# The first stage of an encoder layer: silu's row and the inverse norm in PSUM, three of four latent blocks, the rotary tables and the distances behind the loop

## The chip, the cores and the metric

The kernel runs on one core of a Trainium2 chip. The time is the device time of one execution in microseconds; three executions were measured, and one more was recorded by the hardware profiler. A core has a matrix engine (PE), a vector engine (DVE), an activation engine (ACT), a general engine (POOL) and an engine that issues most DMAs (SP); each works through its own queue of instructions in order, and semaphores tie them together. Data lie in SBUF; PE writes into PSUM, here eight banks of 128 x 512 floats.

## The reference, cut to what matters

Two layers of an encoder on 512 tokens of width 1024, all in float32:

```python
c_act = silu(c)
for l in range(DEPTH):
    mod = c_act @ w_mod[l] + b_mod[l]
    sh1, sc1, gt1, sh2, sc2, gt2 = split(mod, 6)
    h = rms_norm(x, g_norm_mix[l]) * (1 + sc1) + sh1
    q_d, k_d, v_d, cq, ckv, k_rope = split(h @ w_in[l], cuts)
    o_dil = dilated_attention(rms_norm(q_d), rms_norm(k_d), v_d, positions, slopes)   # 8 heads
    o_mla = latent_attention(cq, ckv, k_rope, positions, ...)                         # 8 heads
    x = x + gt1 * (concat([o_dil, o_mla]) @ w_out[l])
    h = rms_norm(x, g_norm_mlp[l]) * (1 + sc2) + sh2
    x = x + gt2 * (relu(h @ w_mlp_in[l]) ** 2 @ w_mlp_out[l])
```

## The kernel before

A product of two float32 matrices is made of three matmuls (`mm3`, L237 to L240): both factors are split into a high and a low half, and high x high, low x high and high x low are added up in PSUM. The high half is a copy on ACT; the low half is the difference, mostly on POOL. `load_split` (L228) does this for weights: a DMA into a "raw" or "zz" tile, ACT's copy (L233, tile wh), POOL's subtraction (L234, tile wl).

Activations lie transposed: x is eight tiles of 128 features by 512 tokens. The projection `w_in` is cut into four pairs of dilated heads, PR[0] to PR[3] (384 columns each), and W, the latent projection (416 columns: query latent, key-value latent, rotary key). Each is done in four blocks of 128 tokens (`tb`), over eight feature tiles (`k`): 24 matmuls of 128x384 or 128x416 to a block.

The first stage, up to the first scores, stands in the code under `if l == 0`, and does four things. (1) silu(c) is spread to all partitions by two matmuls and copied to SBUF as `cb` (L118). (2) The squares of x are added up (tile o), a matmul with ones gives the sum in all partitions, and `inv_rms` makes the inverse norm y in SBUF. (3) A loop over k = 0 to 7 makes column k of the modulation by two multiplications of a 128x1024 weight block with cb, summed along the row (`mod_block`, L170, DVE, one block in a "qk" and one in an "ot" tile), then u = x * y (L706 or L715, DVE, tile pt), its high half h (L719, ACT), the modulated u (L720, ACT) and the low half of h (L722 on POOL for odd k, L710 on DVE for even k); then PE does the step k of PR[0] into four banks named mm, and of W into four named sc and tr: 24 matmuls to a step. (4) Behind the loop stand the chains: norms of q and k of PR[0] (ACT L435, L222, L223, L446; DVE L436, L224 to L226, L443, L447), the same for the latent (ACT L508; DVE L510 to L512), the transposes of both (L455, L523), and the distances between positions for the linear bias (DVE L312 to L322, ACT L321).

Then come eight stages of heads, two heads each. In the first four, a head and block of 128 queries has its scores on PE (L468, L469, bank sc), the softmax with bias on DVE (L343) and ACT (L344, L351), the bias made on ACT (L338) and POOL (L339), the normalisation on POOL (L355) or ACT, transposes on PE (L358, bank tr) and the product with values (L368). The projection of the next pair and its loads and splits are woven in between.

The program is written with a list scheduler that puts each engine's instructions into an order from a simulated time line; where the code names an engine in `manual_schedule` (before: DVE, in the loop alone) or calls `keep_in_program_order`, the order is that of the code. Tiles come from pools with a fixed number of buffers to a name: a new tile waits for the readers of the one whose buffer it takes.

Of the kernel before, what the change touches and what calls it, by code (L numbers as in the profile page):

```python
# [9 lines left out]
F32 = mybir.dt.float32  # L10
# [6 lines left out]
L = 2  # L17
D = 1024
# [24 lines left out]
def trunk(ctx: ExitStack, tc: tile.TileContext, a):  # L43
# [7 lines left out]
    psum = ctx.enter_context(tc.tile_pool(name="psum", bufs=1, space=bass.MemoryType.PSUM))  # L51
# [4 lines left out]
    def nm(p):  # L56
# [5 lines left out]
                mm=4, sc=2, tr=2)  # L62
# [10 lines left out]
    def ps(tag, shape=(128, 512)):  # L73
        return psum.tile(list(shape), F32, tag=tag, bufs=BUFS[tag], name=nm(tag))
# [12 lines left out]
    SY.dma_start(cs, a["c"].rearrange("(k p) -> p k", p=128))  # L87
    ident = const.tile([128, 128], F32, name="ident")
    SY.dma_start(ident, a["ident"])
    cols = [col(N_COL, f"cols{l}") for l in range(L)]  # L90
    SY.dma_start(cols[0], a["cols"][0])
    posc = const.tile([128, 4], I32, name="posc")
    SY.dma_start(posc, a["pos"].rearrange("(t p) -> p t", p=128))
    inv = col(16, "inv")
    SY.dma_start(inv, bass.AP(tensor=a["inv"].tensor, offset=a["inv"].offset, ap=[[0, 128], [1, 16]]))

    xT = [const.tile([128, S], F32, name=f"x{j}") for j in range(8)]
    for j in range(8):
        SY.dma_start(xT[j], a["xT"][j])
    ones = const.tile([128, 128], F32, name="ones")  # L100
# [10 lines left out]
    cb = const.tile([128, D], F32, name="cb")  # L111
    for i in range(2):
        p = ps("sc", (128, 4, 128))
        dg = s2([128, 4, 128])
        for k in range(4):
            V.tensor_scalar(dg[:, k], ident, cs[:, 4 * i + k:4 * i + k + 1], None, op0=OP.mult)
        T.matmul(p.rearrange("p k c -> p (k c)"), ones, dg.rearrange("p k c -> p (k c)"), start=True, stop=True)
        A.activation(cb[:, 512 * i:512 * i + 512], p.rearrange("p k c -> p (k c)"), AF.Copy)  # L118
# [814 lines left out]
```

## Time and profile before

| | |
|---|---|
| median of three executions | 1374.31 us (1374.08 to 1374.61) |
| profiled execution | 1371.87 us, its span 1370.1 us |
| PE busy | 1274.0 us, 93% of the span |
| DVE, ACT, POOL busy | 762.4, 683.7 and 662.0 us |
| mean granted clock | 0.974 |

The profile gives for one execution every instruction with its start, its duration and what ended the idle time before it. The numbers of the instructions' tiles are left out there, so `mm` is any bank of that name; a line (L234) is one of the program above, and may be that of a helper that many parts call. In the lines of the timeline the first column is the start in us, the second the duration (several like instructions in a row are one line, with their count at the end).

### The profile page before, as it was taken

The numbers are of one execution on the slowest core, as the hardware profiler recorded it, in microseconds if no ns is written. First come the engines' busy times: TensorE is split into PE (matmuls) and PEld (weight loads), VectorE is DVE, ScalarE is ACT, GpSimd is POOL, SyncE is SP. The second block draws the span as 40 slices with busy tenths as digits, with TensorE's granted clock in tenths as the row PEclk, the third lists the DMA queues.
The fourth block names the chain that finished last, engine by engine and source line by source line (L and its number), as shares of the span: only waits on it lengthen the run. The fifth ranks groups of instructions, "written<-read, shape, count | busy, mean of one in ns | idle before, by whom it ended". The sixth has DMA issues, their size and how long they took to land.

```text
span 1370.1 us, 19443 instructions
## 1 busy us (share of the span) xinstructions
PE 1274.0 (93%) x6922; PEld 1106.1 (81%) x6922; DVE 762.4 (56%) x1732; ACT 683.7 (50%) x1453; POOL 662.0 (48%) x600
## 2 busy tenths in 40 slices
PE   3889878888999999999998999899889999999999
PEld 2877867777988888888888999788788888888888
DVE  6687887786653481743576577998562122121223
ACT  5578787876442231322235577888654233232321
POOL 5646686663454444444436244455246444444441
PEclk7989998999999999999999999999999999999999
DMA  9325553232235483754533244311013223222321
GB/s 344 112 88 184 165 160 101 87 108 73 98 123 185 149 280 108 235 203 133 181 124 89 89 122 145 93 47 47 17 62 106 94 93 101 99 92 97 104 92 62
DMA packets 57248, 167.61 MB, mean 122 GB/s; under 512 B 8640, under 2 KB 10816, under 8 KB 57152
## 3 DMA queue, kind: packets, MB, share of 16 engines
q1 hardware_dynamic: 57152, 166.38, 37.3%
q8 instruction: 54, 0.88, 0.3%
q14 instruction: 42, 0.34, 0.1%
HBM read 155.87 MB, written 10.49 MB: 121 GB/s over the span
## 4 chain that ended last, share of the span: by engine, by line
PE 73%; DVE 6%; ACT 6%; issue 4%; POOL 3%; DMA 3%; POOLq 0%; DVEq 0%; ACTq 0%
PE mm L238 21%; PE mm L239 21%; PE mm L240 21%; PE tr L368 2%; PE tr L358 2%; POOL wl L234 2%; DMA raw<-in_wout_dram 1%; DVE pt L362 1%; DVE raw L170 1%; DMA raw<-in_wup_dram 1%; ACT pt L361 1%; PE sc L238 1%; ACT P L347 1%; PE mm L603 1%; PE sc L239 1%
## 5 line engine op out<-in xcount | busy, mean ns | idle before, releaser
L234 POOL TENSOR_TENSOR wl<-raw,wh 128x1024 fp32r<-128x1024 f32 (+3 forms) x188 | 425.7, 2268 | 454.9 <-ACT wh L233 433.1
L233 ACT ACTIVATE wh<-raw 128x1024 fp32r<-128x1024 f32 (+3 forms) x188 | 188.7, 1004 | 272.6 <-PE mm L240 202.7
L636 DVE SCALAR_TENSOR_TENSOR x<-mm,mod,x 128x512 f32<-128x512 f32 (+1 forms) x144 | 89.3, 630 | 261.7 <-PE mm L240 261.2
L238 PE MATMUL mm<-h,wh 128*128 128x512 f32 (+1 forms) x608 | 224.5, 370 | 7.1 <-ACT h L274 7.1
L239 PE MATMUL mm<-h,wl 128*128 128x512 f32 (+1 forms) x608 | 224.4, 370 | 0.0
L240 PE MATMUL mm<-h,wh 128*128 128x512 f32 (+1 forms) x608 | 222.1, 369 | 1.6 <-POOL h L271 1.1
L238 PE MATMUL mm<-ot,wh 128*128 128x512 f32 (+1 forms) x448 | 155.2, 348 | 4.3 <-ACT ot L628 4.1
L239 PE MATMUL mm<-ot,wl 128*128 128x512 f32 (+1 forms) x448 | 154.0, 345 | 0.0
L240 PE MATMUL mm<-ot,wh 128*128 128x512 f32 (+1 forms) x448 | 152.6, 347 | 0.2 <-POOL ot L629 0.2
L809 ACT ACTIVATE P<-mm 128x512 f32<-128x512 f32 (+1 forms) x72 | 39.2, 551 | 203.2 <-PE mm L240 203.2
L238 PEld LDWEIGHTS mm<-h,wh 128*128 128x128 f32 x608 | 116.1, 191 | 25.9 <-ACT h L274 7.5
L240 PEld LDWEIGHTS mm<-h,wh 128*128 128x128 f32 x608 | 114.6, 190 | 21.1 <-POOL h L271 1.5
L239 PEld LDWEIGHTS mm<-h,wl 128*128 128x128 f32 x608 | 116.1, 191 | 19.1 <-POOL wl L234 0.3
L810 DVE SCALAR_TENSOR_TENSOR mm<-mm,P 128x512 f32<-128x512 f32 (+1 forms) x72 | 45.4, 635 | 139.5 <-ACT P L809 139.5
L238 PE MATMUL mm<-wh,h 128*128 128x384 f32 (+1 forms) x288 | 97.0, 352 | 16.5 <-ACT h L719 9.8
L238 PE MATMUL mm<-qk,wh 128*128 128x512 f32 (+1 forms) x288 | 105.2, 366 | 1.0 <-DVE x L636 1.0
L239 PE MATMUL mm<-qk,wl 128*128 128x512 f32 (+1 forms) x288 | 105.2, 365 | 0.0
L240 PE MATMUL mm<-qk,wh 128*128 128x512 f32 (+1 forms) x288 | 105.2, 365 | 0.0
L239 PE MATMUL mm<-wh,h 128*128 128x384 f32 (+1 forms) x288 | 99.8, 349 | 5.3 <-POOL h L722 3.2
L240 PE MATMUL mm<-wl,h 128*128 128x384 f32 (+1 forms) x288 | 99.3, 347 | 0.8 <-POOL wl L234 0.8
L170 DVE SCALAR_TENSOR_TENSOR pt<-pt,cb 128x1024 f32<-128x1024 f32 x56 | 99.2, 1806 | 0.0
L238 PEld LDWEIGHTS mm<-ot,wh 128*128 128x128 f32 x448 | 85.3, 190 | 15.2 <-ACT ot L628 4.5
(248 smaller groups left out, 2673.3 us busy)
## 6 DMA issues: line engine op xcount, KB each, us to landing
raw<-in_w_dram SPq DMA_DIRECT2D x64, 512.0 KB, 3.4
pt<-in_wmod_dram SPq DMA_DIRECT2D x56, 512.0 KB, 4.9
raw<-in_w2a_dram SPq DMA_DIRECT2D x48, 512.0 KB, 3.5
raw<-in_wmod_dram SPq DMA_DIRECT2D x24, 512.0 KB, 3.7
raw<-in_win_dram SPq DMA_DIRECT2D x30, 384.0 KB, 3.1
bias<-b SPq DMA_DIRECT2D x32, 256.0 KB, 2.3
raw<-in_wout_dram SPq DMA_DIRECT2D x16, 512.0 KB, 3.7
raw<-in_w2b_dram SPq DMA_DIRECT2D x16, 512.0 KB, 3.3
```

What stands on the lines that cost most here:

```text
L170: r = V.scalar_tensor_tensor(w, w, 1.0, cb, op0=OP.mult, op1=OP.mult, accum_out=out)
L233: A.activation(hi, raw, AF.Copy)
L234: G.tensor_tensor(lo, raw, f(hi), op=OP.subtract)
L238: T.matmul(out, sh, mh, start=first, stop=False)
L239: T.matmul(out, sl, mh, start=False, stop=False)
L240: T.matmul(out, sh, ml, start=False, stop=last)
L347: A.activation(P, sc, AF.Exp, bias=m, scale=1.0, accum_out=l_)
L358: T.transpose(tr[:, kc], P[:, kc * 128:(kc + 1) * 128], ident)
L368: T.matmul(po[:, HALF[qh]], vals(hd, kc), pt[qh][w][:, kc], start=(kc == 0 and w == 0), stop=(kc == 3 and w == 1))
L636: V.scalar_tensor_tensor(xT[j][:, hf], p, gt[:, j:j + 1], xT[j][:, hf], op0=OP.mult, op1=OP.add)
L809: A.activation(r, p, AF.Relu)
L810: V.scalar_tensor_tensor(p, p, 0.0, r, op0=OP.max, op1=OP.mult)
```

## The change

silu's row stays in its two PSUM banks (`cbp`) and is copied to SBUF behind the loop only, by two copies on ACT (L763 of the changed kernel). The inverse norm stays in a bank "y". So the multiplications for the modulation (now L716) and u = x * y (L747) read one operand from PSUM. The sum of squares runs in PSUM as well, and two of the eight squares go to POOL. The banks of the first stage are a pool of its own, closed behind the loop, and a second pool with the old names is opened after that.

With two banks for cb, one for y and four for PR[0], one bank is left for the latent projection: in the loop only its block 0 is done, 15 matmuls to a step in place of 24. The other three blocks, 72 matmuls, stand behind the loop. All sixteen modulation blocks are loaded into eight "qk" tiles; four latent weight halves lie in "ot" tiles. All low halves of h are made on POOL. In the loop the order on SP, DVE, ACT and POOL is that of the code.

Five small loads are issued from ACT's queue; the arithmetic of the rotary angles goes from POOL to DVE; the split of positions into high and low parts moves to the start of the program. The distances use ACT and, in place of one DVE instruction, two on POOL (L329, L330), behind the loop and ahead of the first latent chain. PR[1]'s first two loads with their splits, and the rotary tables, come behind the latent blocks.

```diff
-    psum = ctx.enter_context(tc.tile_pool(name="psum", bufs=1, space=bass.MemoryType.PSUM))
+    start = ExitStack()
+    psum = [start.enter_context(tc.tile_pool(name="psum0", bufs=1, space=bass.MemoryType.PSUM))]
...
+                mm=4, sc=2, tr=2, cb=1, y=1, w=2, lat=1)
...
+    posc = const.tile([128, 4], I32, name="posc")
+    A.dma_start(posc, a["pos"].rearrange("(t p) -> p t", p=128))
+    inv = col(16, "inv")
+    A.dma_start(inv, bass.AP(tensor=a["inv"].tensor, offset=a["inv"].offset, ap=[[0, 128], [1, 16]]))
+    posr = s2([128, S], I32, tag="o")
+    A.dma_start(posr, bass.AP(tensor=a["pos"].tensor, offset=a["pos"].offset, ap=[[0, 128], [1, S]]))
...
-    cb = const.tile([128, D], F32, name="cb")
-    for i in range(2):
-        p = ps("sc", (128, 4, 128))
-        dg = s2([128, 4, 128])
-        for k in range(4):
-            V.tensor_scalar(dg[:, k], ident, cs[:, 4 * i + k:4 * i + k + 1], None, op0=OP.mult)
-        T.matmul(p.rearrange("p k c -> p (k c)"), ones, dg.rearrange("p k c -> p (k c)"), start=True, stop=True)
-        A.activation(cb[:, 512 * i:512 * i + 512], p.rearrange("p k c -> p (k c)"), AF.Copy)
...
+    cbp = ps("cb", (128, D))
+    for i in range(2):
+        dg = s2([128, 4, 128], tag="P")
+        for k in range(4):
+            V.tensor_scalar(dg[:, k], ident, cs[:, 4 * i + k:4 * i + k + 1], None, op0=OP.mult)
+        T.matmul(cbp[:, 512 * i:512 * i + 512], ones, dg.rearrange("p k c -> p (k c)"), start=True, stop=True)
...
+    def split(raw, n, tags=("wh", "wl"), keep=False):
+        hi, lo = t4(tags[0], [128, 1024])[:, :n], t4(tags[1], [128, 1024])[:, :n]
+        ra = A.activation(hi, raw, AF.Copy)
+        rg = G.tensor_tensor(lo, raw, f(hi), op=OP.subtract)
+        if keep:
+            tc.keep_in_program_order(ra)
+            tc.keep_in_program_order(rg)
+        return hi, lo
...
+    def distances(row, clm):
         dist = [t4("ot", [128, 2, S], F32) for _ in range(2)]
         for qb in range(4):
             d = dist[qb // 2][:, qb % 2]
-            A.activation(d, row[:, 0], AF.Identity, bias=clm[:, 0, qb:qb + 1], scale=65536.0)
-            V.scalar_tensor_tensor(d, row[:, 1], clm[:, 1, qb:qb + 1], d, op0=OP.subtract, op1=OP.add)
+            tc.keep_in_program_order(A.activation(d, row[:, 0], AF.Identity, bias=clm[:, 0, qb:qb + 1], scale=65536.0))
+            u = s2()
+            G.tensor_scalar(u, row[:, 1], clm[:, 1, qb:qb + 1], 0.0, op0=OP.subtract, op1=OP.add)
+            G.tensor_tensor(d, d, u, op=OP.add)
...
+            blocks(w, W_C, step, chain, 1 if l == 0 else 0)
...
-            lbanks = [ps("sc") for _ in range(2)] + [ps("tr") for _ in range(2)]
...
+            def mods(k):
+                ml[8 + k] = mod_load(0, 8 + k, "qk")
+                ml[k] = mod_load(0, k, "qk")
...
+            def splits(i):
+                PR[0]["put"](i, *split(wr[i][0], 768))
+                W["put"](i, *split(wr[i][1], 2 * W_C, ("ot", "ot") if i < 2 else ("wh", "wl")))
+            def mod_mul(i):
+                V.scalar_tensor_tensor(ml[i], ml[i], 1.0, cbp, op0=OP.mult, op1=OP.mult, accum_out=mraw[:, i:i + 1])
...
+            with tc.manual_schedule(engines={E.SP, E.DVE, E.Activation, E.Pool}):
...
+                sq0, sqp = s2(tag="o"), ps("lat")
+                A.activation(sqp, xT[0], AF.Square)
+                for j in range(1, 8):
+                    sq = s2(tag="P")
+                    if j in (1, 4):
+                        G.tensor_tensor(sq, xT[j], xT[j], op=OP.mult)
+                    else:
+                        A.activation(sq, xT[j], AF.Square)
+                    V.tensor_tensor(sq0 if j == 7 else sqp, sqp, sq, op=OP.add)
+                T.matmul(p, ones, sq0, start=True, stop=True)
...
+                for k in range(8):
+                    u = us[k // 2][:, k % 2]
+                    hi, lo = hh[k // 2][:, k % 2], hl[k // 2][:, k % 2]
+                    ga, be = amix[0][:, k:k + 1], modc[0][:, k:k + 1]
+                    V.tensor_tensor(u, xT[k], p, op=OP.mult)
+                    first_norm(k)
+                    A.activation(hi, u, AF.Identity, bias=be, scale=ga)
+                    A.activation(u, u, AF.Identity, bias=be, scale=ga)
+                    G.tensor_tensor(lo, u, f(hi), op=OP.subtract)
+                    if k % 2 == 0 and k < 6:
+                        splits(k // 2 + 1)
                     if k < 7:
-                        if k >= 0:
-                            V.tensor_tensor(u_of(k + 1), xT[k + 1], y, op=OP.mult)
-                        mod_block(0, 9 + k, "qk", out=mraw[:, 9 + k:10 + k])
-                    if k >= 0 and k % 2 == 0:
-                        hi, lo = h_of(k)
-                        V.tensor_tensor(lo, u_of(k), f(hi), op=OP.subtract)
-                    if k < 7:
-                        mod_block(0, k + 1, "ot", out=mraw[:, k + 1:k + 2])
-                        if k < 0:
-                            inv_rms(p, v, y, t)
-                            V.tensor_tensor(u_of(0), xT[0], y, op=OP.mult)
-                        first_norm(k + 1)
-                        hi, lo = h_of(k + 1)
-                        ga, be = amix[0][:, k + 1:k + 2], modc[0][:, k + 1:k + 2]
-                        A.activation(hi, u_of(k + 1), AF.Identity, bias=be, scale=ga)
-                        A.activation(u_of(k + 1), u_of(k + 1), AF.Identity, bias=be, scale=ga)
-                        if k % 2 == 0:
-                            G.tensor_tensor(lo, u_of(k + 1), f(hi), op=OP.subtract)
-                    if k >= 0:
-                        for tb in range(4):
-                            PR[0]["step"](banks[tb][:, :384], k, tb)
-                        for tb in range(4):
-                            W["step"](lbanks[tb][:, :W_C], k, tb)
-            gains()
+                        mod_mul(9 + k)
+                        mod_mul(k + 1)
+                    for tb in range(4):
+                        PR[0]["step"](banks[tb][:, :384], k, tb)
+                    W["step"](lbank[:, :W_C], k, 0)
...
             for tb in range(4):
                 PR[0]["do_chain"](tb, banks[tb])
-            for fn in PR[1]["load"][:2]:
-                fn()
-            for tb in range(4):
-                W["do_chain"](tb, lbanks[tb])
+            for i in range(2):
+                tc.keep_in_program_order(A.activation(cb[:, 512 * i:512 * i + 512], cbp[:, 512 * i:512 * i + 512], AF.Copy))
+            bias0 = distances(*parts)
+            W["do_chain"](0, lbank)
+            start.close()
+            psum[0] = ctx.enter_context(tc.tile_pool(name="psum", bufs=1, space=bass.MemoryType.PSUM))
+            for tb in range(3):
+                for fn in W["mm"][tb]:
+                    fn()
             for fn in PR[0]["tail"]:
                 fn()
+            for fn in PR[1]["load"][:2]:
+                fn(keep=True)
+            for tb in range(3):
+                W["chain"][tb]()
             W["tail"]()
-            bias0 = distances()
```

How the instructions stand now is shown at three places; the names are tiles with their numbers, and "waits" lists the semaphores that an instruction waits for (of engines, and of DMA queues).

The first is PE's queue at the end of the loop, in the kernel before: h_191 and wl_490 are low halves, tr_208 and tr_209 banks of the latent projection, pt_576 and pt_605 normalised q and k of PR[0].

```order
L239 MATMUL tr_208<-wh_489,h_191 128x416
L240 MATMUL tr_208<-wl_490,h_190 128x416
L239 MATMUL tr_209<-wh_489,h_191 128x416
L240 MATMUL tr_209<-wl_490,h_190 128x416
L455 MATMUL mm_698<-ident,pt_576 128x128 x4
L455 MATMUL mm_705<-ident,pt_576 128x128 x4
```

And in the changed kernel, where lat_263 is the one latent bank of the loop, mm_598 the first bank of the second pool, and ot_268 and ot_269 latent weights:

```order
L244 MATMUL mm_187<-wh_399,h_163 128x384
L245 MATMUL mm_187<-wl_400,h_162 128x384
L244 MATMUL lat_263<-wh_403,h_163 128x416
L245 MATMUL lat_263<-wl_404,h_162 128x416
L243 MATMUL mm_598<-ot_268,h_156 128x416 [waits DVE_49,PE_49,Activation_49]
L244 MATMUL mm_598<-ot_268,h_157 128x416
L245 MATMUL mm_598<-ot_269,h_156 128x416
```

The transposes of PR[0] stood right behind the loop's last matmul; now the 72 matmuls of three latent blocks stand between, and the first of them waits for the last readers of the first pool, which are the chain of latent block 0.

The second is ACT's queue behind the loop in the changed kernel: qk_495 is a value of PR[0]'s chain, ot_556 and ot_557 are distances, b_819 and b_869 biases, s_579 and st_580 squares of latent block 0 and their sums.

```order
L456 ACTIVATE qk_495<-mm_187 128x2x64 [waits DVE_49]
L763 ACTIVATE cb<-cb_126 128x512 x2
L327 ACTIVATE ot_556<-ot_167,pc_169 128x512 x2
L327 ACTIVATE ot_557<-ot_167,pc_169 128x512 x2
L346 ACTIVATE b_819<-ot_556 128x512 [waits Pool_49]
L346 ACTIVATE b_869<-ot_556 128x512 [waits Pool_49]
L519 ACTIVATE s_579,st_580<-lat_263 128x256 [waits PE_49,Pool_49]
L519 ACTIVATE s_579,st_580<-lat_263 128x128
L519 ACTIVATE s_579,st_580<-lat_263 128x32
L218 ACTIVATE st_584<-st_580,eps_97 128x3 [waits Activation_49]
L219 ACTIVATE lat_263<-st_584 128x3 [waits Activation_49]
```

In the kernel before, the same end of PR[0]'s chain (qk_564) and the first latent chain (sc_206) on ACT:

```order
L446 ACTIVATE qk_564<-mm_204 128x2x64
L223 ACTIVATE mm_205<-st_613 128x4
L459 ACTIVATE qk_562<-mm_705,kcol_192 128x2x256
L508 ACTIVATE s_638,st_639<-sc_206 128x256
L508 ACTIVATE s_638,st_639<-sc_206 128x128
L508 ACTIVATE s_638,st_639<-sc_206 128x32
```

The latent chain followed PR[0]'s directly; the copies of cb, four distances and two biases now stand between, and its first instruction waits for POOL, since it takes a buffer named s that POOL's distances use.

The third is POOL's queue at the end of the loop in the kernel before (rot: rotary tables; wl_484 and wl_490: the last weights of the loop; wl_625, wl_631, wl_829 and wl_835: PR[1]'s; h_191: the last low half of the loop):

```order
L490 TENSOR_SCALAR rot_762<-rot_762 128x4x16
L234 TENSOR_TENSOR wl_484<-zz_482,wh_483 128x768
L234 TENSOR_TENSOR wl_490<-zz_488,wh_489 128x832
L234 TENSOR_TENSOR wl_625<-raw_623,wh_624 128x768
L722 TENSOR_TENSOR h_191<-pt_201,h_190 128x512
L234 TENSOR_TENSOR wl_631<-raw_629,wh_630 128x768
```

and in the changed kernel, where h_163 is the last low half, s_559 to s_571 the buffers named s, and wl_704 PR[1]'s first split:

```order
L751 TENSOR_TENSOR h_163<-pt_183,h_162 128x512 [waits Activation_49] x2
L329 TENSOR_SCALAR s_559<-ot_167,pc_169 128x512 [waits DVE_49,Activation_49]
L329 TENSOR_SCALAR s_563<-ot_167,pc_169 128x512 [waits DVE_49,Activation_49]
L330 TENSOR_TENSOR ot_556<-ot_556,s_559 128x512 [waits Activation_49,Pool_49]
L330 TENSOR_TENSOR ot_556<-ot_556,s_563 128x512 [waits Activation_49,Pool_49]
L329 TENSOR_SCALAR s_567<-ot_167,pc_169 128x512 [waits Pool_49]
L347 TENSOR_TENSOR b_819<-b_819,ot_574 128x512 [waits DMAHW6_49,Activation_49]
L329 TENSOR_SCALAR s_571<-ot_167,pc_169 128x512 [waits Pool_49]
L347 TENSOR_TENSOR b_869<-b_869,ot_574 128x512 [waits Activation_49]
L330 TENSOR_TENSOR ot_557<-ot_557,s_567 128x512 [waits Pool_49]
L330 TENSOR_TENSOR ot_557<-ot_557,s_571 128x512 [waits Pool_49]
L228 TENSOR_TENSOR wl_704<-raw_701,wh_703 128x768 [waits DMAHW3_49,PE_49,Activation_49]
```

PR[1]'s splits and the rotary tables have left the loop; the distances and the first two biases follow the last low half, and the splits come after them.

More of the change, by code (lines that the diff above doesn't have):

```diff
@@ L99, in trunk @@
         SY.dma_start(xT[j], a["xT"][j])
+    cols = [col(N_COL, f"cols{l}") for l in range(L)]
+    A.dma_start(cols[0], a["cols"][0])
     ones = const.tile([128, 128], F32, name="ones")
@@ L160, in trunk, with mod_load, mod_block @@
     amlp = [col(8, f"al{l}") for l in range(L)]
-    def mod_block(l, i, tag="raw", pool_=False, pin=False, out=None):
-        out = modc[l][:, i:i + 1] if out is None else out
+    def mod_load(l, i, tag):
         w = t4(tag, [128, D], F32)
         SY.dma_start(w, a["wmod"][l, i])
+        return w
+    def mod_block(l, i, tag="raw", pool_=False, pin=False):
+        out = modc[l][:, i:i + 1]
+        w = mod_load(l, i, tag)
         if pool_:
@@ L227, in rsqrt_tiny, with load, load_split @@
         return r
-    def load_split(src, n, raw="raw"):
+    def split(raw, n, tags=("wh", "wl"), keep=False):
[6 more added lines that the diff above has]
+        return hi, lo
+    def load(src, n, raw="raw"):
         raw = t4(raw, [128, 1024], F32)[:, :n]
-        hi, lo = t4("wh", [128, 1024])[:, :n], t4("wl", [128, 1024])[:, :n]
         SY.dma_start(raw, src)
-        A.activation(hi, raw, AF.Copy)
-        G.tensor_tensor(lo, raw, f(hi), op=OP.subtract)
-        return hi, lo
+        return raw
+    def load_split(src, n, keep=False):
+        return split(load(src, n), n, keep=keep)
     def mm3(out, sh, sl, mh, ml, first, last):
@@ L317, in distances @@
         V.tensor_scalar(clm[:, 0], clm[:, 0], -65536.0, None, op0=OP.mult)
+        return row, clm
+    def distances(row, clm):
         dist = [t4("ot", [128, 2, S], F32) for _ in range(2)]
@@ L399, in group, with put, load @@
             ws = {}
-            def load(i, raw="raw"):
-                hi, lo = load_split(src[i], 2 * n, raw)
+            def put(i, hi, lo):
                 ws[i] = (hi.rearrange("p (k n) -> p k n", k=2), lo.rearrange("p (k n) -> p k n", k=2))
+            def load(i, keep=False):
+                put(i, *load_split(src[i], 2 * n, keep))
             def step(bank, k, tb):
@@ L407, in step, with blocks @@
                     ws[k // 2][0][:, k % 2], ws[k // 2][1][:, k % 2], k == 0, k == 7)
-            return [lambda i=i, **kw: load(i, **kw) for i in range(4)], step
-        def blocks(w, n, step, chain):
-            for tb in range(4):
+            return [lambda i=i, **kw: load(i, **kw) for i in range(4)], step, put
+        def blocks(w, n, step, chain, first=0):
+            for tb in range(first, 4):
                 st = {}
@@ L424, in dil_prep @@
             w = dict(mm=[], chain=[])
-            w["load"], step = group(a["win"][l, pr], 384)
+            w["load"], step, w["put"] = group(a["win"][l, pr], 384)
             R = {}
@@ L497, in latent @@
             w = dict(mm=[], chain=[])
-            w["load"], step = group(a["winc"][l], W_C)
+            w["load"], step, w["put"] = group(a["winc"][l], W_C)
             def chain(tb, bank):
```

99 lines of the change are left out of this document (43 added, 56 removed).

## The prediction

> **What bounds the kernel now.** I read the page first, then busy time by stretches of the first layer, then groups and the timeline inside the stretches where TensorE (PE) loses time.
>
> ```profile
> span 1370.1 us, 19443 instructions
> PE 73%; DVE 6%; ACT 6%; issue 4%; POOL 3%; DMA 3%; POOLq 0%; DVEq 0%; ACTq 0%
> 0.00:25.39 25.39, 5.79 (x6) 1.67 (x6) 14.75 (x43) 14.15 (x25) 11.53 (x20) 0.73 0.89 321
> 25.39:70.62 45.23, 39.71 (x192) 37.17 (x192) 31.68 (x45) 24.61 (x44) 29.32 (x23) 0.92 0.47 167
> 70.62:81.77 11.15, 6.35 (x22) 4.08 (x23) 10.41 (x36) 8.98 (x41) 2.90 (x2) 0.62 0.41 122
> 81.77:98.77 17.00, 15.19 (x86) 14.72 (x85) 14.13 (x42) 9.77 (x28) 7.09 (x12) 0.95 0.25 74
> 98.77:140.00 41.23, 37.18 (x226) 32.16 (x225) 32.56 (x85) 34.92 (x83) 28.61 (x24) 1.00 0.52 167
> 140.00:180.00 40.00, 36.82 (x230) 34.61 (x231) 33.27 (x88) 30.77 (x74) 26.73 (x20) 1.00 0.53 169
> 180.00:220.00 40.00, 28.01 (x161) 22.32 (x160) 29.61 (x91) 33.19 (x81) 35.45 (x45) 0.83 0.51 163
> ```
>
> The chain that ended last is 73% PE. A stretch row gives length, then busy time (and instructions) of PE, PE weight load, DVE, ACT, POOL, the granted clock, the DMA share and GB/s. The first loop takes 45.2 us for 192 matmuls that need much less: warm ones follow each other by 0.18 us.
>
> ```profile
> 68.05 0.35 PE L240 MATMUL mm<-wl,h 128*128 128x384 f32 x1
> 68.23 0.34 PE L239 MATMUL mm<-wh,h 128*128 128x384 f32 x1
> ```
>
> At that step 192 are 34 us. So the loop can give some 10 us at most unless work leaves it; the change takes 72 matmuls out, and puts them behind it. The chain behind the loop (70.62 to 81.77) leaves PE idle half the time. From 98.77 on PE is over 90% busy up to 180 and 70% after that.
>
> **The start.** The loop begins when u0 and its h are ready:
>
> ```profile
> 23.80 0.69 DVE L715 TENSOR_TENSOR pt<-x,P 128x512 f32<-128x512 f32 x1
> 25.39 0.69 PE L238 MATMUL mm<-wh,h 128*128 128x384 f32 x1 [9.48 <-ACT h L719]
> ```
>
> Afterwards the squares wait for the rotary angles' activation tables on ACT, while two squares go to POOL and the norm loses a few small steps. Five small loads leave SP's queue for ACT's, so x is issued a little earlier on SP. I set this at +0.5 us, between -1 and +1.6.
>
> **The loop.** Its two limits are DVE, which makes the modulation, and POOL, which makes the low halves of weights and h.
>
> ```profile
> L170 DVE SCALAR_TENSOR_TENSOR qk<-qk,cb 128x1024 f32<-128x1024 f32 x7 | 11.5, 1644 | 0.0
> L722 POOL TENSOR_TENSOR h<-pt,h 128x512 fp32r<-128x512 f32 x4 | 6.7, 1686 | 8.6 <-ACT pt L720 8.6
> 30.21 3.01 DVE L170 SCALAR_TENSOR_TENSOR qk<-qk,cb 128x1024 f32<-128x1024 f32 x1
> 49.40 1.22 DVE L170 SCALAR_TENSOR_TENSOR qk<-qk,cb 128x1024 f32<-128x1024 f32 x1
> 105.85 1.29 POOL L339 TENSOR_TENSOR b<-b,ot 128x512 f32<-128x512 f32 x1
> 105.92 0.69 DVE L443 TENSOR_TENSOR zz<-mm,st 128x512 f32<-128x512 f32 x1
> 107.65 1.24 DVE L170 SCALAR_TENSOR_TENSOR raw<-raw,cb 128x1024 f32<-128x1024 f32 x1
> 107.77 2.24 POOL L339 TENSOR_TENSOR b<-b,ot 128x512 f32<-128x512 f32 x1
> ```
>
> The same multiply takes 3.01 us with POOL busy and 1.22 without: with both inputs in SBUF the two engines stop each other. One PSUM input lifts it: L443 (mm is PSUM) ran beside a POOL subtract-type instruction in 0.69 us and POOL in 1.29, while L170 cost POOL 0.95 more. With cb and p in PSUM I therefore take 1.22 and 0.69 per instruction: 2 x 1.22 + 0.69, some 3.1 us a step, and DVE no longer sets the pace. If PSUM operands lift nothing, steps stay at 1.64 a multiply and POOL at 1.69 (the groups' means): the loop is then up to 8 us longer.
>
> POOL has eight h low halves at 1.29 and six weight splits:
>
> ```profile
> 59.15 0.81 ACT L720 ACTIVATE pt<-pt,mod,am 128x512 f32<-128x512 f32 x1
> 60.30 3.81 POOL L234 TENSOR_TENSOR wl<-zz,wh 128x768 fp32r<-128x768 f32 x2
> 64.07 1.84 POOL L234 TENSOR_TENSOR wl<-raw,wh 128x768 fp32r<-128x768 f32 x1
> 65.86 1.30 POOL L722 TENSOR_TENSOR h<-pt,h 128x512 fp32r<-128x512 f32 x1
> ```
>
> Before, x7's low half was ready at 59.96 and ran at 65.86, behind splits, one of them PR[1]'s, which leave the loop now, as do the rotary tables. 8 x 1.3 + 6 x 1.85 = 21.5 us of POOL from 26.7 (the second, 0.81-us form of h0 done behind the start above) give 48.2; the last 15 matmuls of a step stand behind that, and with the waits for earlier splits I put the last matmul of PR[0]'s first bank, T0, at about 51.5 us; before, it is the row at 68.05. Of these 16.5 us, 72 x 0.187 = 13.4 us are only moved. The eight "qk" buffers make loads 9 to 16 wait for multiplies; at the start's 321 GB/s a block of 128x1024 f32 (512 KB) takes 1.6 us, and the last pair lands some 2 us before DVE wants it by this sum, so I count it as just hidden; uncovered, each block costs its 1.6. Bounds for T0: 48 to 57.
>
> **The gap behind it.** The first moved matmul opens a PSUM pool that cannot open before the old one's last reader is through: block 0's latent chain. On ACT this stands behind the 16 steps of PR[0]'s chain, two cb copies, four distance steps and two bias steps; its first square waits in turn for POOL's distances.
>
> ```profile
> 68.07 0.74 ACT L435 ACTIVATE s<-mm 128x256 f32<-128x256 f32 x2 [4.05 <-PE mm L240]
> 77.95 0.28 ACT L446 ACTIVATE qk<-mm 128x128 fp32r<-128x128 f32 x1 [0.46 <-DVE pt L443]
> 7.96 0.58 ACT L118 ACTIVATE cb<-sc 128x512 f32<-128x512 f32 x1
> 90.36 2.58 ACT L321 ACTIVATE ot<-pt,pc 128x512 f32<-128x512 f32 x4
> 99.40 0.69 POOL L355 TENSOR_SCALAR P<-P,hs 128x512 f32<-128x512 f32 x1
> 76.03 0.39 ACT L508 ACTIVATE s<-sc 128x256 f32<-128x256 f32 x1
> 79.37 0.24 DVE L512 TENSOR_SCALAR kr<-sc,st 128x32 f32<-128x32 f32 x1
> 80.33 0.80 PE L468 MATMUL sc<-qk,qk 128*128 128x512 f32 x1 [0.33 <-DVE qk L464]
> ```
>
> PR[0]'s chain took 10.2 us from 68.07 with two weight copies of 0.85 in it: 8.3 without. Two copies of 0.58: 9.4. The first distance step of 0.65: 10.1. From there POOL has five adds at 1.29 and two constant steps at 0.69 ahead of the tile that the square waits for: 7.8, so T0 + 17.9. Latent block 0 took 3.6 us before from its first square to its last result (76.03 to 79.61) with other work mixed in; I take 3.0. So the first moved matmul starts at T0 + 21, at 72.4 us, and PE is idle for some 20 us. No row of before shows POOL taking a constant from a column at this size with two operations; at 0.43 to 1.29 for each such step the gap is 0.5 us shorter or 1.2 longer.
>
> All 72 moved matmuls stand ahead of everything else on PE: 13.5 us, and slow ones after the idle time. The nearest row for that:
>
> ```profile
> 52.93 0.69 PE L239 MATMUL mm<-wh,h 128*128 128x384 f32 x1 [1.85 <-POOL h L722]
> 53.42 0.52 PE L240 MATMUL mm<-wl,h 128*128 128x384 f32 x1
> 53.74 0.52 PE L239 MATMUL mm<-wh,h 128*128 128x384 f32 x1
> ```
>
> Behind a wait of 1.85 us matmuls follow each other by 0.32 us for nine of them, 1.3 us lost; I add 1.3. The Trainium skill (TensorE: Matmul & The Clock Gate, Part 1, What's actually happening) says that after an idle window of about 3.4 us the array runs at half its clock until a window of that length has been busy; that would be an estimated 1.7 us lost here, and the sum would be 0.4 us longer. The row above shows the halved pace after a shorter wait.
>
> The moved matmuls end at T0 + 36, at 87.4. PR[0]'s tail transposes and the scores are queued behind them on PE. Before, 2.4 us passed from the last eviction of that chain (77.95) to the first score (80.33) with most transposes done; with all sixteen still to do I take twice that, 5, so the first scores run at 92.5 against 80.33, **12 us later**.
>
> **What the head stage gives back.** Before, the first softmax did not follow the scores: it waited for the distances and the bias.
>
> ```profile
> 93.72 2.76 POOL L339 TENSOR_TENSOR b<-b,ot 128x512 f32<-128x512 f32 x2 [4.62 <-ACT b L338]
> 95.99 0.68 DVE L343 CUSTOM_DVE_ANT_0 P<-sc,b 128x512 f32<-128x512 f32 x1
> 125.61 0.69 DVE L343 CUSTOM_DVE_ANT_0 P<-sc,b 128x512 f32<-128x512 f32 x1 [0.61 <-PE sc L469]
> L238 PE MATMUL mm<-wh,h 128*128 128x384 f32 x24 | 8.6, 358 | 1.8 <-DVE ot L528 1.8
> ```
>
> Afterwards the bias is made early, and the first softmax comes at about 93.5, 2.5 us earlier than 95.99. But between 80.3 and 98.8 PE did 72 matmuls of PR[1] (24 in each of three such groups), 12.5 us of work that now lies inside the first head stage, together with PR[1]'s loads on SP, its four splits (4 x 1.84 us of POOL) and the rotary tables. So PE stands 12.5 - 2.5 - some 3 us (transposes and projections from the latent that also move) = about 7 us behind at the first softmax. Idle PE in 98.77 to 180 is 4.1 + 3.2 us, and the second of the two stage boundaries (125.61) waits for PE scores, so lateness goes through there. Half or less of the idle time can be used, since it lies in waits that stay: I take 2.5 off, and +0.5 for the start is in the times above already. **Net +5 us**: 1371.9 (the profiled execution, 1.8 us around its span) becomes 1377; the median of the runs is 2.4 us above the profiled execution, which makes 1379.
>
> **Rivals.**
> 1. Faster. POOL's queue, not PE, sets the head stages: 180 to 220 has PE at 28.0 of 40 us and POOL at 35.5. If softmax's pace there decides, PE's debt is worked off in those 12 idle us, and what is left is the earlier first softmax (-2.5) and a loop that ends at POOL's bound of 48 (-3.3). This decides if the debt entering 180 us is under some 8 us and no score waits for a projection: 1366 to 1371, central 1369. Against it: the boundary row at 125.61 waits for PE.
> 2. Nothing to measure. The two cancel within 0.2% (2.7 us, about what a measurement of this kernel can tell from no change): 1372 to 1377.
> 3. The change doesn't do what it says: PSUM operands don't free DVE and POOL, or the eight buffers delay loads. The loop ends up to 8 us later, nothing behind hides that since PE waits for the loop: 1387 to 1390. Against it: the 0.69 beside 1.29 above.
>
> **How the numbers follow.** My case, +2.7 to +12, gets 0.42; rival 3 (slower too) 0.09; rival 2 0.19; rival 1 0.30. So faster 0.30, same 0.19, slower 0.51. The bounds: loop end 48 to 57 (-3.5 to +5.5), POOL's constant steps -0.5 to +1.2, absorption 0 to 7 us. From the central 1379 the range goes down to 1366 for most of rival 1 and up to 1389.
>
> **What would show it.** After the change the multiplies by cb should take 1.15 to 1.25 us each and those by p 0.69, beside POOL rows of 1.3; the loop's last matmul near 51.5; then one idle time of PE of about 20 us, released by DVE's last latent result, with the slow matmuls after it; first softmax near 93.5; PR[1]'s splits behind it; the first softmax of the next stage near 133 where it was 125.6. If PE idles much less than 15 us behind the loop, or the second stage begins before 128, the forecast is wrong on the fast side; if multiplies stay over 1.5 us, rival 3 is right.

## The result, and the profile after

| | before | changed |
|---|---|---|
| median | 1374.46 us (1374.08 to 1375.78, 4 runs) | 1393.59 us (1390.95 to 1394.33, 4 runs) |
| ratio | | 1.0132, 95% interval 1.0116 to 1.0148 |
| span of the profiled execution | 1370.1 us | 1392.1 us |
| first matmul of the loop | 25.39 us | 28.75 us |
| PR[0]'s first bank read by ACT (T0) | 68.07 us | 57.55 us |
| first softmax of head stages 0, 1, 2, 3 | 95.99, 125.61, 163.33, 189.37 us | 102.14, 152.72, 182.87, 219.02 us |

The change costs 19 us, where 5 had been forecast: the sign was right, the size nearly four times too small, and the time lies 4.6 us above the stated range. The loop is shorter, as forecast; all of it and more is lost behind it.

The changed kernel's page, its span and the engines of the chain that ended last, and then its stretches up to the second head stage (columns as before: length, busy time of PE, weight load, DVE, ACT, POOL, granted clock, DMA share, GB/s), cut at the loop's start, its last matmul, the first moved matmul, and the first softmax of stage 0, its last, and the first of stage 1:

```profile
span 1392.1 us, 19466 instructions
PE 73%; ACT 7%; POOL 6%; DVE 5%; issue 5%; DMA 3%; SPq 0%; POOLq 0%; ACTq 0%; DVEq 0%
...
0.00:28.75 28.75, 5.86 (x6) 1.68 (x6) 19.16 (x56) 12.37 (x21) 6.06 (x8) 1.00 0.91 333
28.75:58.93 30.18, 26.49 (x120) 24.28 (x120) 22.28 (x40) 21.61 (x40) 21.31 (x14) 0.94 0.57 210
58.93:80.61 21.68, 0.01 (x1) 0.03 (x1) 7.49 (x29) 8.72 (x29) 15.31 (x10) 0.55 0.06 24
80.61:102.14 21.53, 20.38 (x103) 18.82 (x104) 6.74 (x22) 8.24 (x31) 1.26 (x1) 0.90 0.00 1
102.14:127.21 25.07, 22.45 (x124) 20.28 (x122) 15.02 (x37) 16.70 (x39) 20.82 (x28) 0.93 0.48 147
127.21:152.72 25.51, 20.85 (x119) 19.61 (x120) 15.73 (x38) 14.64 (x34) 13.24 (x8) 0.93 0.50 156
```

Two stretches stand out. From 58.93 to 80.61 PE does nothing at all. And from the last softmax of stage 0 to the first of stage 1 it takes 25.5 us, where the kernel before needed 7.2 (118.45 to 125.61), at a clock of 0.93. The last softmax of stage 0 in the kernel before:

```profile
118.45 0.69 DVE L343 CUSTOM_DVE_ANT_0 P<-sc,b 128x512 f32<-128x512 f32 x1
```

In the loop, the groups of the two multiplications and of the low halves of h (busy time, mean of one in ns, idle time before it), and POOL's constant steps and adds of the distances behind it:

```profile
L716 DVE SCALAR_TENSOR_TENSOR qk<-qk,cb 128x1024 f32<-128x1024 f32 x16 | 18.8, 1210 | 0.0
...
L751 POOL TENSOR_TENSOR h<-pt,h 128x512 fp32r<-128x512 f32 x8 | 10.2, 1281 | 9.3 <-ACT pt L750 7.8 <-PE mm L244 1.5
...
L329 POOL TENSOR_SCALAR s<-ot,pc 128x512 f32<-128x512 f32 x4 | 8.0, 1995 | 8.1 <-DVE st L446 8.1
...
L747 DVE TENSOR_TENSOR pt<-x,y 128x512 f32<-128x512 f32 x8 | 5.4, 678 | 0.0
...
L330 POOL TENSOR_TENSOR ot<-ot,s 128x512 f32<-128x512 f32 x4 | 5.0, 1261 | 1.5 <-ACT ot L327 1.5
```

L716, L747 and L751 have the durations of undisturbed instructions: the two engines no longer stop each other. L329 is another matter: 2.0 us, three times what had been put down.

The timeline around the gap, on PE, ACT and POOL (start, duration, and in brackets the idle time before it and what ended it):

```profile
61.80 3.97 POOL L329 TENSOR_SCALAR s<-ot,pc 128x512 f32<-128x512 f32 x2 [8.08 <-DVE st L446]
67.30 2.49 POOL L330 TENSOR_TENSOR ot<-ot,s 128x512 f32<-128x512 f32 x2 [1.53 <-ACT ot L327]
69.77 2.00 POOL L329 TENSOR_SCALAR s<-ot,pc 128x512 f32<-128x512 f32 x1
71.74 1.26 POOL L347 TENSOR_TENSOR b<-b,ot 128x512 f32<-128x512 f32 x1
72.98 1.99 POOL L329 TENSOR_SCALAR s<-ot,pc 128x512 f32<-128x512 f32 x1
74.94 1.26 POOL L347 TENSOR_TENSOR b<-b,ot 128x512 f32<-128x512 f32 x1
76.16 2.48 POOL L330 TENSOR_TENSOR ot<-ot,s 128x512 f32<-128x512 f32 x2
...
77.45 0.38 ACT L519 ACTIVATE s<-lat 128x256 f32<-128x256 f32 x1 [7.00 <-POOL ot L330]
...
80.61 0.68 PE L243 MATMUL mm<-ot,h 128*128 128x416 f32 x1 [21.68 <-DVE kr L523]
```

Read from the bottom: PE's first moved matmul waits 21.68 us for the latent chain of block 0 (kr); ACT's first instruction of that chain waits 7.0 us for POOL; POOL works through distances and biases without a pause from 67.30.

### The profile page after: what moved, and what is told of

It is laid out like the page before. It is cut to its first block, busy times and chain, and to the rows that moved or that the text cites. A ratio compares the mean times of both kernels' runs of the same rounds, so it can differ in the third digit from the quotient of the medians.

```text
span 1392.1 us, 19466 instructions
## 1 busy us (share of the span) xinstructions
PE 1272.9 (91%) x6922; PEld 1107.2 (80%) x6922; DVE 758.5 (54%) x1735; ACT 684.9 (49%) x1451; POOL 670.2 (48%) x600
## 4 chain that ended last, share of the span: by engine, by line
PE 73%; ACT 7%; POOL 6%; DVE 5%; issue 5%; DMA 3%; SPq 0%; POOLq 0%; ACTq 0%; DVEq 0%
PE mm L244 21%; PE mm L243 21%; PE mm L245 21%; PE tr L376 3%; POOL wl L228 2%; PE tr L366 2%; DMA bias<-b 1%; ACT pt L369 1%; DVE pt L370 1%; PE sc L243 1%; ACT wh L227 1%; ACT P L352 1%; ACT P L355 1%; PE sc L244 1%; PE sc L245 1%
## 5 line engine op out<-in xcount | busy, mean ns | idle before, releaser
L849 DVE SCALAR_TENSOR_TENSOR mm<-mm,P 128x512 f32<-128x512 f32 (+1 forms) x72 | 45.4, 636 | 138.5 <-ACT P L848 138.5
L243 PE MATMUL mm<-wh,h 128*128 128x384 f32 (+1 forms) x300 | 101.4, 353 | 12.3 <-ACT h L749 6.3
L244 PE MATMUL mm<-wh,h 128*128 128x384 f32 (+1 forms) x300 | 105.2, 351 | 4.8 <-POOL h L751 3.7
L245 PE MATMUL mm<-wl,h 128*128 128x384 f32 (+1 forms) x300 | 104.1, 348 | 0.0
```

The costliest lines, as they stand in the source:

```text
L243: T.matmul(out, sh, mh, start=first, stop=False)
L244: T.matmul(out, sl, mh, start=False, stop=False)
L245: T.matmul(out, sh, ml, start=False, stop=last)
L849: V.scalar_tensor_tensor(p, p, 0.0, r, op0=OP.max, op1=OP.mult)
```

## The experiments

All eleven were compared with the kernel before on the same chip; its median in the three groups of runs was 1374.98, 1375.96 and 1374.90 us. Where a run is compared with the changed kernel, the two medians come from different groups; between groups the median of the kernel before moved by up to 1.5 us. The diffs are against the changed kernel.

**Undoing the PSUM part (e4).**

```diff
+        A.activation(cb[:, 512 * i:512 * i + 512], cbp[:, 512 * i:512 * i + 512], AF.Copy)
-                V.scalar_tensor_tensor(ml[i], ml[i], 1.0, cbp, ...
+                V.scalar_tensor_tensor(ml[i], ml[i], 1.0, cb, ...
-                    V.tensor_tensor(u, xT[k], p, op=OP.mult)
+                    V.tensor_tensor(u, xT[k], y, op=OP.mult)
```

> silu's row is copied to SBUF at once and the inverse norm goes to SBUF: both inputs of the multiplications are in SBUF again, all else is as in the changed kernel. If PSUM operands are what keeps DVE and POOL from stopping each other: multiplications of 1.4 to 1.7 us instead of 1.21, low halves of h of 1.5 to 1.7 instead of 1.28, the loop 5 to 8 us longer, and 1398 to 1402 us. If they do nothing: loop as long as in the changed kernel, and 1392 to 1394 us.

Measured: 1408.88 us, ratio to before 1.0256 (1.0232 to 1.0280). The same three groups in this run's trace:

```profile
L717 DVE SCALAR_TENSOR_TENSOR qk<-qk,cb 128x1024 f32<-128x1024 f32 x16 | 31.6, 2012 | 0.0
...
L753 POOL TENSOR_TENSOR h<-pt,h 128x512 fp32r<-128x512 f32 x8 | 15.0, 1874 | 15.3 <-ACT pt L752 15.3
...
L749 DVE TENSOR_TENSOR pt<-x,o 128x512 f32<-128x512 f32 x8 | 11.9, 1484 | 0.0
```

2.01 us against 1.21, 1.87 against 1.28, 1.48 against 0.68: the loop takes 42.3 us instead of 30.2, and its start is 3.7 us later. So the PSUM part does what it says, and is worth more than any expectation had it: 15 us, where 4 to 8 had been expected. What makes the change slow is elsewhere.

**The gap, three ways (e1, e3, e2).** e1 moves one statement, the latent chain of block 0, ahead of the cb copies and the distances:

```diff
+            W["do_chain"](0, lbank)
             for i in range(2):
                 tc.keep_in_program_order(A.activation(cb[...
             bias0 = distances(*parts)
-            W["do_chain"](0, lbank)
```

> Only the place of the latent chain of block 0 changes: it comes right behind PR[0]'s chain, ahead of the two copies of cb and of the distances. Theory 1 (the idle time of PE behind the loop, 21.7 us, is the loss, and it is as long as the chain that the first moved matmul waits for): the wait no longer holds POOL's distances, the gap falls from 23 us to about 11 or 12, and nearly all of that is won: about 1382 to 1385 us instead of 1393.6. Theory 2 (the loss is the work itself: 72 matmuls and PR[1]'s projection now lie where PE is busy anyway, and the first scores are late because of that work): the gap falls just as much, but the head stages take up most of it in other waits (bias, splits, softmax): 1390 us or more.

e3 takes POOL out of the distances:

```diff
-            u = s2()
-            G.tensor_scalar(u, row[:, 1], clm[:, 1, qb:qb + 1], 0.0, op0=OP.subtract, op1=OP.add)
-            G.tensor_tensor(d, d, u, op=OP.add)
+            V.scalar_tensor_tensor(d, row[:, 1], clm[:, 1, qb:qb + 1], d, op0=OP.subtract, op1=OP.add)
```

> The second half of the distances is one DVE instruction each again, in place of two on POOL (a constant step that takes 2.0 us there and an add of 1.26). Theory 1: the latent chain no longer waits for POOL, so the gap is PR[0]'s chain, cb copies, distances on ACT and the latent chain: about 14 to 15 us instead of 23, and the time 1384 to 1387 us. If instead the wait for the chain is not what POOL sets (rival: the scheduler's order on ACT behind it), the gap stays over 19 us and the time over 1390.

e2 leaves the mm banks in a pool that stays open:

```diff
+    main = ctx.enter_context(tc.tile_pool(name="psum", bufs=1, space=bass.MemoryType.PSUM))
     psum = [start.enter_context(tc.tile_pool(name="psum0", bufs=1, space=bass.MemoryType.PSUM))]
...
-        return psum[0].tile(list(shape), ...
+        return (main if tag == "mm" else psum[0]).tile(list(shape), ...
```

> The four banks named mm are a pool that stays open through the whole program; only cb, y and lat are in the first stage's own pool. The moved matmuls then wait for PR[0]'s chain of their bank alone. Theory 1: the gap is 3 to 4 us instead of 23, PR[0]'s chain runs beside the 72 matmuls, and 16 to 20 us are won: 1374 to 1378 us, about the time of the kernel before. Theory 2: 1388 us or more, since the same work follows in the same order.

| | idle time of PE behind the loop | first softmax | first softmax of stage 1 | median |
|---|---|---|---|---|
| changed | 21.7 us | 102.1 | 152.7 | 1393.6 us |
| e1 | 8.6 | 91.5 | 141.3 | 1379.2 (ratio 1.0021 to 1.0049) |
| e3 | 12.6 | 90.7 | 138.5 | 1383.3 (1.0042 to 1.0097) |
| e2 | 2.3 | 83.9 | 139.5 | 1384.8 (1.0048 to 1.0095) |

The first moved matmul in e1, e3 and e2, with PE's idle time before it and what ended it:

```profile
67.50 0.69 PE L243 MATMUL mm<-ot,h 128*128 128x416 f32 x1 [8.55 <-DVE kr L523]
...
69.80 0.69 PE L243 MATMUL mm<-ot,h 128*128 128x416 f32 x1 [12.59 <-DVE kr L521]
...
59.68 0.45 PE L244 MATMUL mm<-ot,h 128*128 128x416 f32 x1 [2.34 <-DVE qk L458]
```

e1 shortens the gap by 13.1 us and the program by 14.4, e3 by 9.1 and 10.3. So the gap is lost time, nearly microsecond for microsecond, and theory 2 falls for them; both are 1 to 3 us faster than theory 1 had them. But e2, with the shortest gap of the three, lies between its two theories and is no faster than e1: 19.4 us were won at the gap, 18.2 at the first softmax, and 8.8 at the end. Its stage 0, from its first softmax to that of stage 1, takes 55.6 us, the longest of all runs. Its view of what PE waited for between 59 and 100 us (what, total, times, longest):

```profile
PE sc L479 <- DVE hs L352: 4.5, 3, 3.6
PE mm L466 <- DVE qk L475: 2.8, 2, 1.4
PE mm L244 <- DVE qk L458: 2.3, 1, 2.3
```

After the first scores PE waited for softmax (hs). There was work in the program to fill these waits, PR[1]'s projection, but it had not begun. The loads of its first weights had been issued by 41 us, but their splits ran from 82.3 us on, since ACT's copies stood behind PR[0]'s tails. That made a second cause, with a test of its own.

**PR[1]'s splits (e6, e5, e10).** e6 is the changed kernel with one statement moved:

```diff
             for tb in range(4):
                 PR[0]["do_chain"](tb, banks[tb])
+            for fn in PR[1]["load"][:2]:
+                fn()
...
-            for fn in PR[1]["load"][:2]:
-                fn(keep=True)
```

> The changed kernel with PR[1]'s first two loads and splits ahead of the distances, and nothing else. Theory 1: the gap stays, or grows by up to 4 us if the two splits stand ahead of the distances on POOL, and the weights weren't what PE waited for there: 1390 to 1398 us. Rival (the late weights are a loss by themselves): 1386 us or less with the gap as it was.

Measured: 1387.94 us (ratio 1.0067 to 1.0098), 5.7 us faster, with the gap longer (24.3 us) and the first softmax later (104.1 us). The time lies between the two expectations (1390 and more, 1386 and less), nearer to the rival's: late weights are a loss by themselves. PR[1]'s first split in the changed kernel, and its second in e6, on POOL:

```profile
100.88 3.64 POOL L228 TENSOR_TENSOR wl<-raw,wh 128x768 fp32r<-128x768 f32 x2 [22.24 <-ACT wh L227]
...
58.14 1.80 POOL L228 TENSOR_TENSOR wl<-raw,wh 128x768 fp32r<-128x768 f32 x1 [2.56 <-ACT wh L227]
```

Stage 0 from its first softmax to stage 1's, in the changed kernel and then in e6:

```profile
102.14:152.72 50.58, 43.30 (x243) 39.89 (x242) 30.75 (x75) 31.34 (x71) 34.07 (x35) 0.93 0.49 152
```

```profile
104.06:145.11 41.05, 38.33 (x239) 36.33 (x238) 29.20 (x74) 29.51 (x67) 24.57 (x21) 1.00 0.46 144
```

Almost the same number of matmuls takes 50.6 us in the one and 41.1 in the other: 5.0 us less busy time, at a clock of 1.00 instead of 0.93, and 4.6 less idle time. An estimate from these rows: 43.30 x 0.93 = 40.3, so the clock accounts for some 3 of the 5.0 us. The timelines show what differs: the order that the list scheduler made for PE. Where the first splits are ready early, PR[1] goes block by block, each laid between softmaxes. In the changed kernel each new weight tile is used on three blocks at once as soon as it comes; so PE ran projections in one lump up to 117 us, and then had only the softmax chain to follow. In e6, projection matmuls (mm) stand between transposes:

```profile
124.39 0.28 PE L376 MATMUL tr<-pt,qk 128*128 128x256 f32 x1
124.50 0.34 PE L243 MATMUL mm<-wh,h 128*128 128x384 f32 x1
...
126.55 0.60 PE L366 MATMUL tr<-ident,P 128*128 128x128 f32 x4
126.91 0.42 PE L244 MATMUL mm<-wh,h 128*128 128x384 f32 x1
```

And PE's timeline in that stretch of the changed kernel:

```profile
117.22 0.34 PE L245 MATMUL mm<-wl,h 128*128 128x384 f32 x1
117.39 0.60 PE L366 MATMUL tr<-ident,P 128*128 128x128 f32 x4
118.67 0.50 PE L478 MATMUL sc<-qk,qk 128*128 128x512 f32 x1 [0.68 <-DVE hs L351]
...
120.41 0.50 PE L478 MATMUL sc<-qk,qk 128*128 128x512 f32 x1 [1.00 <-DVE hs L351]
...
122.48 0.71 PE L478 MATMUL sc<-qk,qk 128*128 128x512 f32 x1 [0.90 <-DVE hs L351]
...
128.56 1.31 PE L366 MATMUL tr<-ident,P 128*128 128x128 f32 x8 [1.39 <-DVE o L379]
...
131.97 0.63 PE L366 MATMUL tr<-ident,P 128*128 128x128 f32 x4 [1.14 <-ACT st L218]
...
135.22 0.52 PE L243 MATMUL mm<-wh,h 128*128 128x384 f32 x1
135.54 0.52 PE L244 MATMUL mm<-wh,h 128*128 128x384 f32 x1
```

Short waits without a filler, and matmuls 0.32 us apart after them. PE waited for POOL nowhere in stage 0 of the changed kernel, so POOL's work there (34.07 us, 24.57 in e6) did not hold PE directly; once, for 1.6 us, a softmax waited for POOL's bias.

All runs fall into two groups by this one property. With PR[1]'s splits late (changed, e1, e2, e3, e4, e7, e11) stage 0 takes 47.8 to 55.6 us, at a clock of 0.82 to 0.96. With them early (e5, e6, e8, e9, e10) it takes 40.9 to 41.3, at 1.00.

e5 puts e2, e3 and e6 together.

> The two pools of run e2, the distances' second half on DVE as in e3, and PR[1]'s first two loads and splits ahead of the distances instead of behind the latent blocks. In e2 the gap went to 2.3 us and the first softmax came 18 us earlier, but PE was idle for 5.6 of the 16 us behind the first scores, and PR[1]'s splits ran from 82 us on, behind PR[0]'s tails on ACT. Theory 1b (with the gap gone, PR[1]'s late weights are the next wait): the projection of PR[1] follows the first scores without a pause, the second head stage starts at 125 to 130 us instead of 139.5, and the time is 1370 to 1376 us. Rival (the head stage is held by softmax's chain or by POOL, not by the weights): second stage at 136 or later, and 1381 us or more.

Measured: 1371.16 us, ratio 0.9961 (0.9947 to 0.9976), below the kernel before. Stage 1 starts at 129.9, 23 us earlier than in the changed kernel, and stage 0 takes 40.9 us. What e3's part adds to the other two was not run apart. The gap is 7.6 us and not e2's 2.3: on ACT the scheduler put one of PR[1]'s copies (0.84 us), the two of cb (1.07), the four distances (2.56) and two biases (1.15) between the steps of PR[0]'s chain; another copy of PR[1] stood ahead of it, at 51.55.

e10 is e1 with e6.

> Runs e1 and e6 together: the latent chain of block 0 ahead of the distances, and PR[1]'s two loads ahead of them too; one first-stage pool and POOL's distances as in the changed kernel. If the two losses are separate (the gap behind the loop; the head stage's projection in one lump because PR[1]'s weights are split late), their gains add up: 1393.6 - 14.4 - 5.7, some 1373 us (1371 to 1376). If they are one loss seen twice: 1379 or more, as e1.

Measured: 1379.26 us (1.0021 to 1.0040): the sum did not come, and the time is that of the other case, e1's. But it is not one loss seen twice. Stage 0 is short (98.3 to 139.4, 41.1 us, against 49.8 in e1), so the second loss is gone. But the gap is 12.7 us instead of e1's 8.6, and from the first moved matmul to the first softmax it takes 26.7 us instead of 24.0. With PR[1]'s copies moved, one of them, the two copies of cb and the four distances (0.84, 1.07 and 2.55 us on ACT) ran between the steps of PR[0]'s chain. So of the 8.7 us won in stage 0, 6.8 had been lost ahead of its first softmax, and the last 1.9, by which stage 1 began earlier, did not show at the end. The losses have separate places, and one move does not act on one alone.

**POOL's constant step (e11).**

```diff
-            G.tensor_scalar(u, row[:, 1], clm[:, 1, qb:qb + 1], 0.0, op0=OP.subtract, op1=OP.add)
+            G.tensor_scalar(u, row[:, 1], onec, clm[:, 1, qb:qb + 1], op0=OP.mult, op1=OP.add)
```

(with the column negated once at the start, and onec a column of ones)

> The changed kernel with POOL's four constant steps of the distances (L329, 2.0 us each, subtract and add) written as multiply by a column of ones and add of the negated column, the pair of operations that L363 has, which takes 0.70 us at the same size. If the pair of operations sets the price: 0.65 to 0.80 us each, the gap 2 to 3 us shorter (two of the four stand in the chain that PE waits for), 1390 to 1392 us. If it is something else (the input's place, the two columns): 2.0 us again and 1393 to 1394.

Measured: 1389.12 us (1.0076 to 1.0118), the gap 19.2 us. Of this run, the constant steps on POOL:

```profile
L332 POOL TENSOR_SCALAR s<-ot,one,pc 128x512 f32<-128x512 f32 x4 | 3.1, 770 | 8.9 <-DVE st L449 8.9
```

0.77 us in place of 2.0 with the same input, output and size. L363 has, like L329, a column and a constant, and takes 0.70 us; so it is not the second column that makes it cheap, and the pair of operations sets the price here.

**The start (e7, e8).** e7 puts squares and sums ahead of the angles and their table loads:

```diff
+    sq0, sqp = s2(tag="o"), ps("lat")
+    tc.keep_in_program_order(A.activation(sqp, xT[0], AF.Square))
...
     pf = col(4, "pf")
...
+                inv_rms(p, v, t)
                 gains()
-                inv_rms(p, v, t)
```

> The changed kernel with the start in another order: on ACT the squares of x come ahead of the angle functions and their two table loads, on DVE silu and the sums of squares ahead of the angles, and the small gains behind the inverse norm. Theory 1 (all that PE waits for in the first 29 us is on the path): PE starts at 25 to 27 us instead of 28.75, and the time falls by as much: 1390 to 1392 us. Rival (the later part of the loop is paced by the loads of the modulation, so an earlier start is lost again): loop end within 0.5 us of before, 1393 to 1394 us.

Measured: 1402.34 us (1.0169 to 1.0203), 8.7 us slower. The edit did not do what it was for: the sum of squares came at 20.1 us, as in the changed kernel (20.4), because the first addition on DVE still stood behind the row of positions and behind silu (it began at 11.73), and ACT's second square began only at 12.46; and the angle chain with its two table loads then stood between the sum and the inverse norm, so PE began at 33.55. Of these 4.8 us the loop's end shows 1.7 (it takes 27.1 us instead of 30.2), and the first softmax 2.0. So the loop's end follows its start only in part. The first softmax of stage 1 is 4.0 us later; the rest of the 8.7 us lies behind it, and its cause was not followed and stays open. Neither theory was tested as meant.

> Runs e5 and e7 together. Theory 1: what e7 gains comes on top of e5, some 2 to 3 us: 1367 to 1373 us, under the kernel before. Rival: the start is hidden by the loads, and the time is e5's within 1 us.

e8 is e5 with e7: 1374.50 us (0.9975 to 1.0001), 3.3 above e5 and so outside both expectations, with PE's start at 32.57 and the first softmax 1.5 us later.

**The last step (e9)**, e5 with ACT and POOL held to the code's order for PR[0]'s chain:

```diff
+            with tc.manual_schedule(engines={E.Activation, E.Pool}):
                 for tb in range(4):
                     PR[0]["do_chain"](tb, banks[tb])
+                for fn in PR[1]["load"][:2]:
+                    fn()
```

> As run e5, but on ACT and POOL PR[0]'s chain stands in the code's order ahead of PR[1]'s copies and of cb's; in e5 they had been put ahead of it, and the gap was 7.6 us where e2 had 2.3. Theory 1 (every us of PE's idle time behind the loop counts): the gap is 2 to 4 us, and the time 3 to 5 us under e5: 1366 to 1369 us. Rival (at this point the head stage sets the pace, and its own waits take it back): within 1.5 us of e5, 1370 to 1373 us.

Measured: 1369.88 us, ratio 0.9950 (0.9933 to 0.9967). The gap fell from 7.6 to 2.1 us, but the first softmax moved by 2.0 us only and the time by 1.3, about as the rival had it. Its PE then waited elsewhere, in this view of what PE waited for between 50 and 90 us:

```profile
PE mm L464 <- DVE qk L473: 3.4, 1, 3.4
PE mm L245 <- POOL h L750: 2.1, 1, 2.1
PE mm L244 <- DVE qk L456: 2.1, 1, 2.1
PE mm L464 <- DVE qk L469: 1.6, 1, 1.6
```

5.0 us now lie at the transposes of PR[0]'s tail (L464). It is the fastest version of this study, by the medians 5 us under the kernel before and 24 under the changed one; e5 and e9 can't be told apart by their intervals.

## Why the prediction was wrong, point by point

The way of the loss was forecast: one long wait of PE behind the loop, released by the latent chain's kr, then slow matmuls, then PR[1]'s work in the first head stage. The table takes the terms up to the first softmax of stage 1, which had been put near 133 and came at 152.7.

| term | forecast | measured | difference |
|---|---|---|---|
| PE's start | 25.9 | 28.75 | +2.9 |
| start to T0 | 25.6 | 28.8 | +3.2 |
| T0 to the first moved matmul | 21 | 23.1 | +2.1 |
| from there to the first softmax | 21.1 | 21.5 | +0.4 |
| stage 0, to stage 1's first softmax | 39.5 | 50.6 | +11.1 |

- **Start: mis-sized.** +0.5 had been set, between -1 and +1.6; it was +3.4. The prediction named the wait of the squares for the angles' tables, and made it too short: ACT waited 4.45 us for DVE's angle arithmetic and then loaded two tables of 1.28 us ahead of the first square, which began at 13.24 us (6.73 before). And the small gains took DVE for 1.1 us just when the sum of squares was ready.
- **Loop: mechanism right, shown by e4.** Multiplications 1.21 and 0.68 us, low halves 1.28. T0 came at 57.55, 0.6 us outside the bounds (48 to 57). Of the 6.0 us by which it is later than the forecast 51.5, 2.9 come from the start and 3.2 from the loop. There POOL's 14 instructions took 21.3 us, against 21.5 in the sum, but POOL waited 1.5 and 1.2 us ahead of two of the low halves, and the sum up to 48.2 held no such waits.
- **Gap: right, its inner price wrong.** The releasing chain and the length held within 10%. The constant steps were put at 0.69 from L355's row, with 0.43 to 1.29 as ends; they took 2.0, since L355 multiplies and adds and L329 subtracts and adds (e11). Two of them ran while ACT was still in PR[0]'s chain, which hid half of the error.
- **Slow matmuls after the gap: mis-sized.** Twelve followed each other by 0.35 us, up to 84.9, so for 4.3 us; at 0.19 for a warm step some 2 us were lost, where 1.3 had been added. The Trainium skill (TensorE: Matmul & The Clock Gate, Part 1, What's actually happening) gives an estimated 1.7 by its window of about 3.4 us. The trace agrees with the halved pace (0.35 against 0.19), and has it last 0.9 us longer than that window.
- **What the head stage gives back: the step that failed.** It said that PE stands "about 7 us behind at the first softmax" and that 2.5 of them would be absorbed: PR[1]'s projection was counted as 12.5 us of work, its splits as POOL time, and neither as something that sets an order. The prediction had listed the splits behind the distances, and did not ask when the first weights would be ready, nor in which order PE would then take the matmuls. e6 shows the price: with PR[1]'s splits early stage 0 takes 41.1 us, close to the forecast 39.5; with them late 50.6. This term alone is 11.1 of the 19.6 us by which stage 1 began later than forecast. At the end of the program early splits alone were worth 5.7 us (e6), since the gap grew by 2.6.

From there to the end 5 us were given back (27.1 us late at stage 1, 22.0 at the end of the span); 7.4 late and 5 at the end had been forecast, so that part held in kind. The range failed because its ends moved only the loop, POOL's constant steps and the absorption; the length of stage 0 had no term of its own.

Rival 1, that POOL's pace in the head stages works PE's debt off, is refuted by e1 and e3: what the gap gave came through to the end. In e2 and e9, with the gap nearly gone, part of it does not come through: there other waits of PE begin to decide. Rival 2, nothing to measure, falls with the interval of 1.0116 to 1.0148. Rival 3 is refuted by the loop's rows and e4.

## What to carry to other kernels

When work is moved behind a stage to make that stage shorter, look first at what its first instruction must wait for: here a closing pool joined a matmul to the slowest chain of the stage, and one statement moved (e1) won 14 of the 19 us. Then look at the weights of the next stage: a projection costs what its matmuls take only if its operands come early enough to spread it between the waits of the stage that it fills; late ones came in a lump here, and the waits behind it stayed empty. And a price taken from another row needs the same pair of operations and not only the same shape: here the two prices were 0.70 and 2.00 us.

## What the runs showed of the hardware that had not been expected

- POOL's two-operation instruction with a column, 128x512 float32: multiply and add 0.70 us (L363 of the changed kernel) or 0.77 with two columns (e11), subtract and add 2.00 us.
- In e4, where DVE was busy for 37.5 of the loop's 42.3 us, DVE and POOL stopped each other by more than in the kernel before (31.7 of 45.2 us): with both inputs in SBUF the multiplication of 128x1024 took 2.01 us on average (e4), with one in PSUM 1.21, and POOL's subtraction 1.87 and 1.28. Before, they were 1.64 in the qk group (1.39 in the ot group) and 1.69. That DVE's share of the time is the reason was not tested.
